# A two-layer hybrid trunk on one core: dense projections in pairs of k, a new price list for the order, first weights loaded earlier

## The chip, the cores and the metric

The kernel runs on one core of one Trainium2 chip. The metric is the device time of one execution in microseconds (us); lower is better. The kernel before takes 2569.01 us, the median of 3 runs (2567.93 to 2573.7).

The profile names the engines: PE is TensorE's matmul, PEld its weight load, DVE is VectorE, ACT is ScalarE, POOL is GpSimd and SP is SyncE, which issues the DMAs (SPq is its queue).

## The reference

The program is a trunk of two layers over 2048 positions of width 1024, in fp32. In each layer:

```python
h = rms_norm(x, norm_g[l]) * (1.0 + scale[:, None]) + shift[:, None]
proj = h @ w_in[l]
gq, gk, gv, glr, gz, dq, dk, dv, dz = split_columns(proj)
...
o_gla = gla_branch(gq, gk, gv, glr, gz, ...)      # 4 heads, linear attention by chunks of 64
o_diff = diff_branch(dq, dk, dv, dz, ...)         # 4 heads, two softmax maps, block-causal
y = jnp.concatenate([o_gla, o_diff], axis=-1) @ w_out[l]
x = x + gate[:, None] * y
```

`shift`, `scale` and `gate` come from `silu(c) @ w_ada[l] + b_ada[l]` and are called the modulation here. `gq`, `gk` and `gv` pass a causal convolution of 4 taps and a SiLU.

## The kernel before

**Units.** Each layer is cut into four units of 512 positions, u = 0 to 3. A unit has seven dense items, each of 8 k-tiles of 128 rows: items 0 to 3 are the four attention heads' projections (`proj_N`, the h tile is stationary), 4 and 5 the convolved inputs of the linear attention (`proj_T`, the weight is stationary), 6 its gate. Items 7 and 8 are the two halves of the output projection (`out_gen`). To keep fp32 accuracy with fast matmuls every operand is split into a high and a low part of type fp32r, and each product takes three matmuls: high by high, high by low, low by high. One k-tile of an item is 12 matmuls of 512 columns, an item is 96, and an item needs all four accumulator banks (`ps_a`, tiles named acc) until they are evacuated.

**Weights.** `weights()` gives the split weight of one k-tile in a tile w, of which there are four buffers (`p_w`). The first time (u = 0) the raw rows are loaded into tiles named raw, two k-tiles in one tile of the pool `p_kv` (5 buffers, shared with the keys Kj and Kt); ACT makes the high part, DVE the low part, and the result is kept in DRAM. Later units load the kept 512 KB (w<-wd).

**Attention.** For each of the four 128-row query tiles of a head: the scores (tiles sc, from Kj of earlier units and Kt of this one) are copied to s with a running minimum, ACT takes the exponential, DVE combines the two maps, PE transposes s (tp<-ident,s), ACT copies the transposes to aT, and PE multiplies aT by the values (po<-Vj,aT). At the end the four results are transposed (tp<-ident,z) and split into oh and ol for the output projection. A unit u works on u+1 blocks of keys, so u = 3 is the longest.

**Start.** `start()` loads the first layer's modulation weights in four chunks of 2 MB (`ada_load`, tiles wr) and turns each chunk, with the four x tiles, into two k-tiles of h (tp<-wr,cact, sc<-sel,t and tp<-ident,xt).

**What sets the order.** Generators (`dense_stream`, `attn_stream`, `gla_stream` and others) write the operations down in a program order. `Program.order()` then plays the program through with the durations of `cost()` and the latencies of `LAT`: an engine that is free takes, among the operations that are ready by these prices, the one that stands first in program order. The result is the fixed instruction order of each engine; on the chip an engine works through it in order and waits where something isn't ready. All instructions are issued at line 306 (`issue`), so the trace is read by tile names, not by lines.

In `dense_stream` the output projection of the unit before comes first, then the dense items of this one; for u = 0 they go in the order 0, 4, 1, 5, 2, 3, 6. `out_gen` takes the heads in the order

```python
for n_, k in enumerate((4, 5, 6, 0, 1, 2, 3, 7)):
    yield need("oT", key, 0 if k < 4 else k, lag=0.8)
```

so that 7 of its 8 k-tiles, 84 matmuls of the first half, need nothing of the last attention head (k = 7).

Of the kernel before, what the change touches and what calls it, by code (L numbers as in the profile page):

```python
# [11 lines left out]
F32 = mybir.dt.float32  # L12
# [15 lines left out]
EPS = 1e-6  # L28
NEG = -1e30
C_GQ, C_GV, C_GLR, C_GZ, C_D = 0, 512, 1024, 1040, 1552  # L30

# [87 lines left out]
class Program:  # L119
# [51 lines left out]
    @staticmethod  # L171
    def cost(e, method, args, kw, out):
        n = math.prod(out.shape[1:])
        if e == "S":
            return math.prod(out.shape) * 4 / 360.0
        if e == "T":
            if method == "transpose":
                return 110
            rate = {F32R: 2.4, BF16: 2.4, F32: 0.6}[args[2].dt]
            if rate == 0.6 and args[1].shape[1] < P:  # L180
                return 78
            return max(n / rate, 107 * args[1].shape[1] / P if rate == 2.4 else 216) + 3
        ins = [a for a in list(args[1:]) + list(kw.values()) if isinstance(a, View) and a is not kw.get("accum_out")]
        scalars = sum(math.prod(a.shape[1:]) == 1 for a in ins) if n > 1 else 0
        psum = any(a.buf.psum for a in ins)
        if method == "tensor_reduce":
            n = math.prod(ins[0].shape[1:])
        if e == "A":
            return 0.834 * n + (52 if psum else 93) + 93 * (scalars + ("accum_out" in kw))
        if e == "G":  # L190
            return 300 + 165 * n if kw.get("op") == ALU.pow else 100 + 2.2 * n
        fast = method in ("tensor_copy", "tensor_scalar") and not psum
        return (0.52 if fast else 1.042) * n + 68 + 61 * scalars

# [5 lines left out]
    def order(self):  # L200
# [25 lines left out]
        work, win = {}, 3413  # L226
        res, burst = [], 0
        while len(res) < N:
# [41 lines left out]
            elif e == "A" and self.table(ops[i]) not in (None, table):  # L270
                table = self.table(ops[i])
                free[e] = end = t + ops[i][5] + 1283
            elif e == "T":
                w = int(t / win)
                warm = work.get(w - 1, 0.0) > 0.5 * win
# [34 lines left out]
def trunk_kernel(ctx, tc, x, c, w_ada, b_ada, norm_g, w_in, conv_w, w_gk, b_gk, gla_norm_g,  # L310
# [238 lines left out]
    def pe(cost, wait=0.0):  # L549
        return ("pe", cost, wait)  # L550
# [34 lines left out]

    raws = {}

    def weights(l, u, item, k, src, n=None):
# [7 lines left out]
        if k % 2 == 0:  # L596
            raws[k // 2] = p_kv.tile([P, 2, 512], F32, tag="K", name="raw")
            for j in range(2):
                raw = raws[k // 2][:, j, :]
                SY.dma_start(raw if n is None else raw.rearrange("p (g n) -> p g n", n=n), src(k + j))  # L600
        raw = raws[k // 2][:, k % 2, :]
# [73 lines left out]
    def start():  # L675
# [6 lines left out]
        alloc_h()  # L682
        for c in range(4):
            if c < 3:
                wr.append(ada_load(c + 1))
            ada_first(c, wr[c])
            for pr in range(2):
                make_h(0, xs[2 * pr:2 * pr + 2], pr, c)
# [3 lines left out]
    def proj_T(l, u, item, col, banks):  # L692
        hhi, hlo = state["hhi"], state["hlo"]
        for k in range(KT):
            hi, lo = weights(l, u, item, k, lambda k: w_in[l, k * P:(k + 1) * P, col:col + 512])
            for j in range(4):
                cs = slice(j * P, (j + 1) * P)
                if k == 0:
                    banks.append(acc())
                T.matmul(banks[j], hi[:, cs], hhi[k], start=(k == 0), stop=False)  # L700
                T.matmul(banks[j], hi[:, cs], hlo[k], start=False, stop=False)
                T.matmul(banks[j], lo[:, cs], hhi[k], start=False, stop=(k == KT - 1))
                yield pe(0.65)

# [5 lines left out]
    def proj_N(load, banks):  # L710
        hhi, hlo = state["hhi"], state["hlo"]
        for k in range(KT):
            hi, lo = load(k)
            for t in range(TT):
                ts_ = slice(t * P, (t + 1) * P)
                if k == 0:
                    banks.append(acc())
                mm3(banks[t], hhi[k][:, ts_], hlo[k][:, ts_], hi, lo, k == 0, k == KT - 1)
                yield pe(0.65)

# [370 lines left out]
    def dense_gen(l, u, items):  # L1091
# [12 lines left out]
        def head_proj(hd):  # L1104
            def src(k):
                cols = w_in[l, k * P:(k + 1) * P, C_D:C_D + 2048].rearrange("p (g n) -> p g n", n=512)
                return cols[:, :, hd * P:hd * P + P]

            def ld(k):
                return weights(l, u, hd, k, src, n=P)  # L1110

            banks = []
            yield from proj_N(ld, banks)
            if hd == LAST:
# [34 lines left out]
    def out_gen(l, u):  # L1149
# [3 lines left out]
        final = key == L * NU - 1  # L1153
        yield need("ada", l, 2)
        for hf in range(2):
            cs = slice(hf * 512, hf * 512 + 512)
# [52 lines left out]
    def dense_stream():  # L1209
        order = (0, 4, 1, 2, 5, 3, 6)  # L1210
        prev = None
        for l in range(L):
            for u in range(NU):
                yield need("h", l * NU + u, lag=2.0)
                if prev:
                    yield from out_gen(*prev)
                yield from dense_gen(l, u, (0, 4, 1, 5, 2, 3, 6) if u == 0 else order)
                prev = (l, u)
# [47 lines left out]
```

## Time and profile before

| | |
|---|---|
| median of 3 runs | 2569.01 us |
| the profiled execution | 2571.75 us |
| its span, first to last instruction | 2570.0 us |
| PE busy | 2483.7 us (97%) |
| PEld busy | 2037.7 us (79%) |
| DVE busy | 1741.6 us (68%) |
| ACT busy | 1279.4 us (50%) |
| mean granted TensorE clock | 0.993 |
| DMA, mean over the span | 184 GB/s |

The stages stand on the time axis like this: start until about 32 us; layer 0, u = 0 until about 284; its units 1 to 3 until about 1284; the output projection of unit 3 until about 1340; layer 1, u = 0 until about 1540; its other units until 2540; the last 30 us are the rest of the last output projection. A matmul's recorded duration is longer than the distance to the next one's start, since matmuls are pipelined; so PE's busy share says where it clearly stood still, and hides short waits.

### The profile page before, as it was taken

The page shows a single profiled execution, that of the slowest core. Times are in us where ns is not written, and L with a number is a line of the kernel's source. Part 1 is how long each engine was busy: PE and PEld are TensorE (multiplying, and loading weights), DVE is VectorE, ACT ScalarE, POOL GpSimd, SP SyncE. Part 2 cuts the span into 40 slices and gives each one's busy share as a digit, 9 for nine tenths or more (in the row PEclk, how much of TensorE's full clock was granted, in tenths as well). Part 3 has the DMA queues.
Part 4 walks back from the last instruction along what each step waited for, and adds up shares of the span by engine and source line. Part 5 has one row for each costly group of instructions (what it writes and reads, how often), then busy time and mean ns, then how long its engine had stood idle before and what let it go on. Part 6 is the DMA issues. An engine that isn't in the chain of part 4 may idle for free.

```text
span 2570.0 us, 40465 instructions
## 1 busy us (share of the span) xinstructions
PE 2483.7 (97%) x13923; PEld 2037.7 (79%) x13923; DVE 1741.6 (68%) x5313; ACT 1279.4 (50%) x2760; POOL 139.7 (5%) x424
## 2 busy tenths in 40 slices
PE   8998999999999999999899999999999999999997
PEld 5776788777888878888777777888788888888886
DVE  4788777772777737677748883667637776377763
ACT  5556534562445624556625663445624556255532
POOL 0001000000000000000000010000000000000000
PEclk9999999999999999999999999999999999999998
DMA  8668866456453564434277567444464444643342
GB/s 257 236 225 289 300 232 219 132 187 228 149 189 101 187 212 146 141 131 167 94 260 264 214 226 260 161 165 173 145 237 160 145 154 150 229 138 129 108 147 90
DMA packets 204685, 474.00 MB, mean 184 GB/s; under 512 B 20736, under 2 KB 82368, under 8 KB 204480
## 3 DMA queue, kind: packets, MB, share of 16 engines
q1 hardware_dynamic: 204480, 471.41, 53.2%
q8 instruction: 111, 1.82, 0.3%
q14 instruction: 94, 0.77, 0.1%
HBM read 360.19 MB, written 111.15 MB: 183 GB/s over the span
## 4 chain that ended last, share of the span: by engine, by line
PE 76%; DVE 12%; ACT 6%; DMA 3%; issue 2%; SPq 1%; POOL 0%; ACTq 0%; POOLq 0%; DVEq 0%
PE acc L306 50%; PE sc L306 10%; PE po L306 9%; PE tp L306 7%; DVE s L306 5%; ACT qh L306 2%; DVE t L306 1%; ACT s L306 1%; DVE w L306 1%; DMA raw<-in_w_in_dram 1%; DVE ql L306 1%; DVE Kt L306 1%; ACT t L306 1%; ACT Kt L306 1%; SPq L306 1%
## 5 line engine op out<-in xcount | busy, mean ns | idle before, releaser
L306 PE MATMUL acc<-w,hhi 128*128 128x512 f32 x2560 | 831.3, 402 | 1.9 <-DVE w L306 1.1
L306 PEld LDWEIGHTS acc<-w,hhi 128*128 128x128 f32 x2560 | 465.1, 189 | 92.3 <-ACT ub L306 3.7
L306 PE MATMUL acc<-w,hlo 128*128 128x512 f32 x1280 | 505.3, 396 | 0.0
L306 ACT ACTIVATE s<-s,mx 128x256 f32<-128x256 f32 (+15 forms) x256 | 307.9, 1203 | 333.4 <-DVE s L306 328.9
L306 PE MATMUL acc<-hhi,w 128*128 128x512 f32 x1024 | 369.0, 404 | 0.2
L306 PE MATMUL acc<-w,oh 128*128 128x512 f32 x1024 | 334.3, 401 | 1.6 <-ACT oh L306 1.6
L306 DVE TENSOR_SCALAR_CACHE_REDUCE s<-sc,mx 64x64 f32<-64x64 f32 (+5 forms) x640 | 306.5, 485 | 35.7 <-PE sc L306 17.7
L306 PEld LDWEIGHTS acc<-w,hlo 128*128 128x128 f32 x1280 | 241.3, 188 | 49.2
L306 PEld LDWEIGHTS acc<-w,oh 128*128 128x128 f32 x1024 | 190.9, 190 | 42.9 <-issue 2.5
L306 PEld LDWEIGHTS acc<-hhi,w 128*128 128x128 f32 x1024 | 192.3, 189 | 38.4 <-DVE z L306 2.3
L306 PE MATMUL po<-Vj,aT 128*128 128x128 f32 x1536 | 209.5, 281 | 12.8 <-ACT aT L306 12.1
L306 PEld LDWEIGHTS po<-Vj,aT 128*128 128x128 f32 x1536 | 196.1, 196 | 25.4 <-ACT aT L306 19.0
L306 ACT COPY aT<-tp 128x512 f32<-128x512 f32 (+2 forms) x320 | 161.4, 520 | 104.6 <-PE tp L306 101.7
L306 PE MATMUL acc<-w,ol 128*128 128x512 f32 x512 | 202.7, 398 | 0.0
L306 PE MATMUL acc<-hlo,w 128*128 128x512 f32 x512 | 202.2, 395 | 0.0
L306 DVE SCALAR_TENSOR_TENSOR s<-s,r 128x512 f32<-128x512 f32 (+2 forms) x320 | 197.9, 668 | 3.4
L306 PE MATMUL tp<-ident,s 128*128 128x128 f32 x1088 | 174.0, 276 | 23.8 <-DVE s L306 7.8
L306 DVE TENSOR_SCALAR_CACHE_REDUCE s<-sc 128x512 f32<-128x512 f32 (+4 forms) x256 | 157.9, 622 | 55.5 <-PE sc L306 50.9
L306 PEld LDWEIGHTS tp<-ident,s 128*128 128x128 f32 x1088 | 131.4, 141 | 64.0 <-issue 24.7
L306 ACT COPY rw<-acc 128x256 f32<-128x256 f32 x128 | 50.3, 393 | 221.7 <-PE acc L306 220.5
L306 PE MATMUL sc<-Kj,qh 128*128 128x512 f32 x384 | 157.7, 411 | 2.2 <-DVE Kt L306 1.0
L306 ACT ACTIVATE qh<-tp,G 64x512 fp32r<-64x512 f32 x128 | 87.4, 683 | 128.3 <-PE tp L306 105.5
(183 smaller groups left out, 3708.5 us busy)
## 6 DMA issues: line engine op xcount, KB each, us to landing
w<-wd SPq DMA_DIRECT2D x424, 512.0 KB, 3.7
wd<-w SPq DMA_DIRECT2D x144, 512.0 KB, 4.2
raw<-in_w_in_dram SPq DMA_DIRECT2D x120, 256.0 KB, 5.3
Kj<-kd SPq DMA_DIRECT2D x48, 512.0 KB, 4.4
wr<-in_w_ada_dram SPq DMA_DIRECT2D x128, 128.0 KB, 2.8
kd<-Kt SPq DMA_DIRECT2D x24, 512.0 KB, 3.3
Vj<-vd SPq DMA_DIRECT2D x48, 256.0 KB, 3.5
wr<-in_w_ada_dram SPq DMA_DIRECT2D x8, 1024.0 KB, 11.9
```

The lines of the kernel that those rows point to most:

```text
L306: getattr(self.engines[e], method)(*[real(a) for a in args], **{k: real(v) for k, v in kw.items()})
```

## The change

Five things are edited.

- `proj_T` and `proj_N` take the k-tiles in pairs: the weights of two k-tiles are fetched first, then each of the four banks gets the six matmuls of both. `out_gen` keeps single k-tiles.
- `cost()` has other numbers, for PE, ACT and DVE (a surcharge for ACT and DVE operations on 64 partitions or fewer, among others), and `order()` adds time when PE changes between full-size matmuls and those of 64x64 or 32 columns.
- The raw weights of head 0, layer 0, are loaded in `start()`, one pair of k-tiles ahead of each later chunk of the modulation.
- In unit 3 of each layer the output projection stands in program order behind the last attention head (`need("attn", key, 3)`).
- The order of the items in u = 0 is 0, 1, 4, 5, 2, 3, 6, and in layer 1, u = 0, items 0 and 1 stand ahead of the output projection of layer 0's unit 3.

```diff
+KS = ((0, 1), (2, 3), (4, 5), (6, 7))
...
             rate = {F32R: 2.4, BF16: 2.4, F32: 0.6}[args[2].dt]
             if rate == 0.6 and args[1].shape[1] < P:
-                return 78
-            return max(n / rate, 107 * args[1].shape[1] / P if rate == 2.4 else 216) + 3
+                return 54 if args[1].shape[0] == CH else 60
+            return max(n * 0.444, 112 * args[1].shape[1] / P) if rate == 2.4 else max(n / rate, 216) + 6
...
+        half = 112 if out.shape[0] <= 64 and n > 16 else 0
...
-        return (0.52 if fast else 1.042) * n + 68 + 61 * scalars
+        return (0.52 if fast else 1.042) * n + 70 + 61 * scalars + half + 30 * ("accum_out" in kw)
...
+                if self.mode(ops[i]) != mode:
+                    mode = self.mode(ops[i])
+                    t += 160 if mode else 190
...
+    def load_raw(k, src, n):
+        raw = p_kv.tile([P, 2, 512], F32, tag="K", name="raw")
+        for j in range(2):
+            r = raw[:, j, :]
+            SY.dma_start(r if n is None else r.rearrange("p (g n) -> p g n", n=n), src(k + j))
+        return raw
...
         for c in range(4):
+            early[c] = load_raw(2 * c, head_src(0, 0), P)
             if c < 3:
                 wr.append(ada_load(c + 1))
             ada_first(c, wr[c])
...
     def proj_N(load, banks):
         hhi, hlo = state["hhi"], state["hlo"]
-        for k in range(KT):
-            hi, lo = load(k)
+        for ks in KS:
+            ws = [load(k) for k in ks]
             for t in range(TT):
                 ts_ = slice(t * P, (t + 1) * P)
-                if k == 0:
+                if ks[0] == 0:
                     banks.append(acc())
-                mm3(banks[t], hhi[k][:, ts_], hlo[k][:, ts_], hi, lo, k == 0, k == KT - 1)
-                yield pe(0.65)
+                for k, (hi, lo) in zip(ks, ws):
+                    mm3(banks[t], hhi[k][:, ts_], hlo[k][:, ts_], hi, lo, k == 0, k == KT - 1)
+                    yield pe(0.65)
...
         yield need("ada", l, 2)
+        if u == NU - 1:
+            yield need("attn", key, 3)
...
                 yield need("h", l * NU + u, lag=2.0)
+                items = (0, 1, 4, 5, 2, 3, 6) if u == 0 else order
+                ahead = 2 if l and u == 0 else 0
+                if ahead:
+                    yield from dense_gen(l, u, items[:ahead])
                 if prev:
                     yield from out_gen(*prev)
-                yield from dense_gen(l, u, (0, 4, 1, 5, 2, 3, 6) if u == 0 else order)
+                yield from dense_gen(l, u, items[ahead:])
```

The order that comes out of it differs on every engine. Three places are shown, each before and after. A name is a tile, without its number; x8 says that a row stands for eight equal ones.

The first is SP's queue at the start, from the small gate weights (t<-in_w_in_dram) on: wr are the modulation's chunks, raw the weights of head 0. Before:

```order
L306 DMA t_240<-in_w_in_dram 128x8x16
L306 DMA wr_245<-in_w_ada_dram 128x8x256
L306 DMA raw<-in_w_in_dram 128x4x128 x4
L306 DMA wr_282<-in_w_ada_dram 128x8x256
L306 DMA wr_314<-in_w_ada_dram 128x8x256
L306 DMA raw<-in_w_in_dram 128x4x128 x4
```

After:

```order
L319 DMA t_227<-in_w_in_dram 128x8x16
L319 DMA raw<-in_w_in_dram 128x4x128 x2
L319 DMA wr_248<-in_w_ada_dram 128x8x256
L319 DMA wr_260<-in_w_ada_dram 128x8x256
L319 DMA raw<-in_w_in_dram 128x4x128 x2
L319 DMA wr_307<-in_w_ada_dram 128x8x256
L319 DMA wr_347<-in_w_ada_dram 128x8x256
L319 DMA raw<-in_w_in_dram 128x4x128 x6
```

Two more raw loads stand further up, ahead of the second chunk. Before the last chunk (the last two rows of wr) four raw loads were issued, now six.

The second is PE at the end of layer 0, from the last score matmuls of head 3 of unit 3 on (sc are scores, tp<-ident,s the transposes, po the product with the values, acc the dense matmuls). Before:

```order
L306 MATMUL sc<-Kt,qh 128x512
L306 MATMUL sc<-Kt,ql 128x512
L306 MATMUL tp<-ident,s 128x128 x10
L306 MATMUL po<-Vj,aT 128x128 x4
L306 MATMUL tp<-ident,s 128x128 x4
L306 MATMUL po<-Vj,aT 128x128 x4
L306 MATMUL tp<-ident,s 128x128
L306 MATMUL po<-Vj,aT 128x128 x4
L306 MATMUL po<-Vt,aT 128x128 x3
L306 MATMUL tp<-ident,s 128x128 x8
```

After:

```order
L319 MATMUL tp<-ident,s 128x128 x8
L319 MATMUL acc<-w,hlo 128x512
L319 MATMUL acc<-w,hhi 128x512 x2
L319 MATMUL acc<-w,hlo 128x512
L319 MATMUL acc<-w,hhi 128x512 x2
L319 MATMUL acc<-w,hlo 128x512
L319 MATMUL acc<-w,hhi 128x512
L319 MATMUL tp<-ident,s 128x128 x3
L319 MATMUL po<-Vj,aT 128x128 x4
L319 MATMUL tp<-ident,s 128x128 x4
```

Matmuls of layer 1's head 0 (acc<-w,hhi and acc<-w,hlo) now stand between the attention's steps. From the one po<-Vt,aT that ends the first query tile's product to the last tp<-ident,z, PE had 15 dense matmuls in its row before, and has 71 now.

The third is PE at the end of the program, in the last attention head's last query tile; acc<-w,oh and acc<-w,ol are the last output projection. Before:

```order
L306 MATMUL sc<-Kt,qh 128x512
L306 MATMUL sc<-Kt,ql 128x512
L306 MATMUL tp<-ident,s 128x128 x12
L306 MATMUL po<-Vj,aT 128x128 x8
L306 MATMUL tp<-ident,s 128x128 x3
L306 MATMUL po<-Vj,aT 128x128 x4
L306 MATMUL po<-Vt,aT 128x128 x3
```

After:

```order
L319 MATMUL tp<-ident,s 128x128 x8
L319 MATMUL acc<-w,oh 128x512
L319 MATMUL acc<-w,ol 128x512
L319 MATMUL acc<-w,oh 128x512 x2
L319 MATMUL acc<-w,ol 128x512
L319 MATMUL acc<-w,oh 128x512 x2
L319 MATMUL acc<-w,ol 128x512
L319 MATMUL acc<-w,oh 128x512 x2
L319 MATMUL acc<-w,ol 128x512
L319 MATMUL acc<-w,oh 128x512 x2
L319 MATMUL acc<-w,ol 128x512
L319 MATMUL acc<-w,oh 128x512
```

Fifteen dense matmuls now stand between the eighth and the ninth transpose. From the first query tile's po<-Vt,aT to the last tp<-ident,z no dense matmul stood in the row before, and 45 stand there now; ahead of that place, in the same head, 84 stood before and 39 stand now. Behind it both have the same 108.

## Rows read from the trace of the kernel before

**Rows 1.** The page: busy time, share of the span and instructions of each engine; and the chain that ended last, as shares of the span.

```profile
PE 2483.7 (97%) x13923; PEld 2037.7 (79%) x13923; DVE 1741.6 (68%) x5313; ACT 1279.4 (50%) x2760; POOL 139.7 (5%) x424
...
PE 76%; DVE 12%; ACT 6%; DMA 3%; issue 2%; SPq 1%; POOL 0%; ACTq 0%; POOLq 0%; DVEq 0%
```

**Rows 2.** The stretches of the program: from:to in us, length, then the busy time (and instructions) of PE, PEld, DVE, ACT and, where it worked, POOL, then the granted PE clock, the DMA share and GB/s.

```profile
0.00:32.00 32.00, 19.98 (x148) 11.81 (x149) 13.38 (x57) 15.10 (x33) 3.57 (x14) 1.00 1.02 320
32.00:284.00 252.00, 238.70 (x1275) 187.32 (x1274) 204.55 (x634) 156.19 (x383) 18.45 (x54) 0.97 0.68 238
284.00:1240.00 956.00, 941.61 (x5363) 781.66 (x5362) 657.61 (x2003) 470.40 (x977) 48.07 (x146) 1.00 0.53 180
1240.00:1300.00 60.00, 53.42 (x302) 41.72 (x301) 32.41 (x89) 28.04 (x50) 3.01 (x10) 0.97 0.39 122
1300.00:1340.00 40.00, 40.00 (x180) 33.00 (x179) 16.79 (x40) 11.13 (x28) 0.00 (x0) 1.00 0.68 258
1340.00:1560.00 220.00, 205.48 (x1109) 160.71 (x1109) 185.08 (x553) 140.44 (x339) 19.13 (x52) 0.99 0.66 235
1560.00:2500.00 940.00, 928.35 (x5285) 775.94 (x5284) 605.75 (x1872) 442.38 (x926) 45.26 (x144) 1.00 0.48 166
2500.00:2540.00 40.00, 29.86 (x169) 24.40 (x168) 20.03 (x62) 15.73 (x27) 2.20 (x5) 0.87 0.04 14
2540.00:2570.00 30.00, 26.24 (x108) 21.17 (x108) 5.98 (x9) 0.00 (x0) 0.00 (x0) 0.94 0.55 193
```

**Rows 3.** Two pieces of the chain in order of time: start, length, what, count.

```profile
299.61 27.35 PE acc L306 x120
...
597.09 47.26 PE acc L306 x208
```

**Rows 4.** Who PE waited for, over the whole span: us in total, times, longest.

```profile
PE sc L306 <- DVE Kt L306: 16.8, 18, 2.2
PE po L306 <- ACT aT L306: 15.2, 14, 3.1
```

**Rows 5.** PE's timeline at the start: start, length, instruction, count, in brackets the idle time before and its releaser.

```profile
31.46 2.31 PE L306 MATMUL acc<-w,hhi 128*128 128x512 f32 x5
...
40.20 1.07 PE L306 MATMUL tp<-wr,cact 128*32 128x256 f32 x16
...
42.90 0.53 PE L306 MATMUL tp<-ident,xt 128*128 128x128 f32 x3
```

**Rows 6.** SP's queue in the same stretch: start, length of the issues, what, count.

```profile
20.99 5.14 SPq L306 DMA_DIRECT2D raw<-in_w_in_dram  x4
26.23 4.14 SPq L306 DMA_DIRECT2D wr<-in_w_ada_dram  x2
```

**Rows 7.** PE waiting for Kt in two stretches, from 32 to 284 us and from 1340 to 1560 us, as in rows 4.

```profile
PE sc L306 <- DVE Kt L306: 7.1, 5, 2.2
...
PE sc L306 <- DVE Kt L306: 5.2, 5, 2.0
```

**Rows 8.** PE's timeline around one such wait: the last transposes of rw, which start the making of Kt, the last dense matmul, and the first score matmul.

```profile
193.16 0.88 PE L306 MATMUL tp<-ident,rw 128*128 128x128 f32 x6
...
197.09 0.39 PE L306 MATMUL acc<-w,hlo 128*128 128x512 f32 x1
199.34 0.33 PE L306 MATMUL sc<-Kt,qh 128*128 128x128 f32 x1 [1.86 <-DVE Kt L306]
```

**Rows 9.** PE's timeline at the end of layer 0.

```profile
1254.60 0.40 PE L306 MATMUL acc<-w,ol 128*128 128x512 f32 x1
1256.48 0.66 PE L306 MATMUL tp<-ident,s 128*128 128x128 f32 x4 [1.48 <-ACT aT L306]
...
1260.54 0.71 PE L306 MATMUL po<-Vt,aT 128*128 128x128 f32 x4 [1.30 <-ACT aT L306]
...
1283.31 0.33 PE L306 MATMUL tp<-ident,z 128*128 128x128 f32 x1 [1.04 <-DVE z L306]
1284.42 1.22 PE L306 MATMUL acc<-w,oh 128*128 128x512 f32 x2 [0.78 <-ACT oh L306]
```

**Rows 10.** The first 80 us of layer 1's u = 0, columns as in rows 2.

```profile
1340.00:1420.00 80.00, 73.03 (x355) 58.41 (x355) 67.20 (x206) 45.07 (x111) 5.88 (x20) 1.00 0.79 273
```

**Rows 11.** PE's timeline at the end of the program.

```profile
2498.58 0.39 PE L306 MATMUL acc<-w,ol 128*128 128x512 f32 x1
...
2504.16 1.78 PE L306 MATMUL tp<-ident,s 128*128 128x128 f32 x12 [0.53 <-DVE s L306]
2508.92 3.02 PE L306 MATMUL po<-Vj,aT 128*128 128x128 f32 x16 [2.98 <-ACT aT L306]
...
2524.19 3.78 PE L306 MATMUL po<-Vj,aT 128*128 128x128 f32 x16 [3.15 <-ACT aT L306]
...
2538.74 0.33 PE L306 MATMUL tp<-ident,z 128*128 128x128 f32 x1 [1.51 <-DVE z L306]
2539.84 1.55 PE L306 MATMUL acc<-w,oh 128*128 128x512 f32 x4 [0.78 <-ACT oh L306]
```

**Rows 12.** DMA issues from 284 to 2500 us: count, KB each, median us from issue to landing.

```profile
w<-wd SPq DMA_DIRECT2D x419, 512.0 KB, 3.7
...
Kj<-kd SPq DMA_DIRECT2D x48, 512.0 KB, 4.4
```

More of the change, by code (lines that the diff above doesn't have):

```diff
@@ L188, in cost @@
         if e == "A":
-            return 0.834 * n + (52 if psum else 93) + 93 * (scalars + ("accum_out" in kw))
+            return 0.834 * n + (45 if psum else 85) + 93 * (scalars + ("accum_out" in kw)) + half
         if e == "G":
@@ L192, in cost, with mode @@
         fast = method in ("tensor_copy", "tensor_scalar") and not psum
-        return (0.52 if fast else 1.042) * n + 68 + 61 * scalars
+        return (0.52 if fast else 1.042) * n + 70 + 61 * scalars + half + 30 * ("accum_out" in kw)
+    @staticmethod
+    def mode(op):
+        if op[1] == "transpose" or op[2][2].dt != F32:
+            return 0
+        k, m = op[2][1].shape
+        return 1 if (k, m) == (CH, CH) else 2 if m == 32 else 0
     @staticmethod
@@ L584, in run_streams, with head_src, src @@
                 clock[0] = max(min(nxt), clock[0]) + 1e-6
-    raws = {}
+    raws, early = {}, {}
+    def load_raw(k, src, n):
[4 more added lines that the diff above has]
+        return raw
+    def head_src(l, hd):
+        def src(k):
+            cols = w_in[l, k * P:(k + 1) * P, C_D:C_D + 2048].rearrange("p (g n) -> p g n", n=512)
+            return cols[:, :, hd * P:hd * P + P]
+        return src
     def weights(l, u, item, k, src, n=None):
@@ L596, in weights @@
         if k % 2 == 0:
[L597 to L600, printed above, removed]
+            raws[k // 2] = early.pop(k // 2) if k // 2 in early else load_raw(k, src, n)
         raw = raws[k // 2][:, k % 2, :]
@@ L693, in proj_T @@
         hhi, hlo = state["hhi"], state["hlo"]
-        for k in range(KT):
-            hi, lo = weights(l, u, item, k, lambda k: w_in[l, k * P:(k + 1) * P, col:col + 512])
+        for ks in KS:
+            ws = [weights(l, u, item, k, lambda k: w_in[l, k * P:(k + 1) * P, col:col + 512]) for k in ks]
             for j in range(4):
                 cs = slice(j * P, (j + 1) * P)
-                if k == 0:
+                if ks[0] == 0:
                     banks.append(acc())
-                T.matmul(banks[j], hi[:, cs], hhi[k], start=(k == 0), stop=False)
-                T.matmul(banks[j], hi[:, cs], hlo[k], start=False, stop=False)
-                T.matmul(banks[j], lo[:, cs], hhi[k], start=False, stop=(k == KT - 1))
-                yield pe(0.65)
+                for k, (hi, lo) in zip(ks, ws):
+                    T.matmul(banks[j], hi[:, cs], hhi[k], start=(k == 0), stop=False)
+                    T.matmul(banks[j], hi[:, cs], hlo[k], start=False, stop=False)
+                    T.matmul(banks[j], lo[:, cs], hhi[k], start=False, stop=(k == KT - 1))
+                    yield pe(0.65)
     def mm3(bank, ahi, alo, hi, lo, first, last):
@@ L711, in proj_N @@
         hhi, hlo = state["hhi"], state["hlo"]
-        for k in range(KT):
-            hi, lo = load(k)
+        for ks in KS:
+            ws = [load(k) for k in ks]
             for t in range(TT):
                 ts_ = slice(t * P, (t + 1) * P)
-                if k == 0:
+                if ks[0] == 0:
                     banks.append(acc())
-                mm3(banks[t], hhi[k][:, ts_], hlo[k][:, ts_], hi, lo, k == 0, k == KT - 1)
-                yield pe(0.65)
+                for k, (hi, lo) in zip(ks, ws):
+                    mm3(banks[t], hhi[k][:, ts_], hlo[k][:, ts_], hi, lo, k == 0, k == KT - 1)
+                    yield pe(0.65)
     def to_oT(blocks, gain):
@@ L1104, in head_proj @@
         def head_proj(hd):
[L1105 to L1110, printed above, removed]
             banks = []
-            yield from proj_N(ld, banks)
+            yield from proj_N(lambda k: weights(l, u, hd, k, head_src(l, hd), n=P), banks)
             if hd == LAST:
```

2 lines of the change are left out of this document (1 added, 1 removed).

## The prediction

> **What bounds the kernel.** I read the page's busy shares first: PE 97%, and PE carries 76% of the chain that ended last [rows 1]. So the kernel is bound by TensorE, and the matmuls of the reference, the same 12,187 in both orders, set a floor that the change can't move. What it can move is PE's standing still. The second view is the table of stretches [rows 2]: the length of a stretch less PE's busy time is its plain idle time. That gives 12.0 us in the first 32, 13.3 in layer 0's first unit (32 to 284), 14.4 in 284 to 1240, 6.6 at the layer boundary (1240 to 1300), none in 1300 to 1340, 14.5 in layer 1's first unit (1340 to 1560), 11.7 in 1560 to 2500, 10.1 in 2500 to 2540 and 3.8 behind it: 86 us in all. The reader is to see that the losses sit in four short places and hardly in the long middle.
>
> The third view is the chain in order of time: 120 dense matmuls in 27.35 us, 208 in 47.26, so 0.227 us each at full rate [rows 3]. I price a dense matmul that fills a gap at that. Since the recorded duration is longer than this distance, waits shorter than about 0.2 us don't show as idle; the true loss is larger than 86 us, by how much no view says. The last view is who PE waited for: Kt, the split key, 18 times with 16.8 us, and aT, the copied transposes, 14 times with 15.2 us [rows 4]. In both the fixed order has put PE at an instruction whose operand comes later than the price list thought, with too few dense matmuls ahead of it.
>
> **Start.** Before the last chunk's transposes (until 43.4 us, [rows 5]) PE's row holds 26 dense matmuls before and 44 now, so 18 x 0.227 = 4.1 us of work is done earlier. Against it, two more raw loads stand ahead of the last modulation chunk. SP's queue took 5.14 us for four of them [rows 6], 1.28 each, so the chunk comes 2.6 us later; by the mean rate of the stretch, 320 GB/s [rows 2], 0.52 MB take 1.6 us. Net 1.5 to 2.5 us gained; I take 2. The ends are 4.1 gained (the later chunk is covered) and 2.6 lost (PE has no gap there for the earlier matmuls).
>
> The raw rows of a head arrive in pieces of 512 bytes, and their four issues held the queue for 5.14 us [rows 6]. The Trainium skill (Perfetto Trace Analysis, DMA Optimizations) says that transfers under 2 KB carry a significant overhead each, which speaks against putting them ahead of the modulation. By that rule the price is the 2.6 and the term 1.5; by the mean rate it is 1.6 and the term 2.5.
>
> **Layer 0, first unit.** Here every weight is split on ACT and DVE, and DVE is busy 204.6 of 252 us [rows 2]. 7.1 of the 13.3 idle us are five waits for Kt [rows 7]. In the shown one the transposes start at 193.16 and the first score at 199.34, with dense matmuls only until 197.09 [rows 8]. Counting the matmul time that each order puts between a head's last rw transpose and its first score, the four heads had 2.0, 2.0, 3.4 and 2.8 us and have 2.0, 3.2, 4.1 and 2.7. So the new prices (a surcharge for operations on 64 partitions, as Kt's are) give back 1.8 us, not 7. With the other waits of the stretch I take 3 gained. Ends: 7.1 gained, and 5 lost if the two heads in a row, 0 and 1, crowd DVE.
>
> **Layer boundary.** In 1240 to 1300 PE stands still 6.6 us. The dense matmuls that need nothing of the last head run out near 1254.60; behind it come the waits of 1.48 and 1.30 us for aT, and at the end 1.04 for z and 0.78 for oh [rows 9]. The order now has 71 dense matmuls in this piece where it had 15: 56 x 0.227 = 12.7 us of filler for 4.8 us of idle (the 6.6 less the last two waits, which also shrink since layer 1's matmuls stand there). The granted clock of the stretch is 0.97 [rows 2], so some 3.6 of its 60 us went at the lower level. I take 6 gained, between nothing (the filler itself waits for its raw weights) and 8.4.
>
> **Layer 1, first unit.** Idle 14.5 us, 7.0 of them in its first 80 us [rows 2, 10], where heads 0 and 1 begin. Their weights are now split during unit 3's attention, where DVE is busy 54% and, to 1340, 42%, not 84% [rows 2], and the output projection, whose weights are kept ones, is left as filler for these two heads. I take the 7.0, between 10 gained and 2 lost (the splits get in the way of unit 3's attention).
>
> **End of the program.** From 2498.58 to 2539.84 no dense matmul stands in PE's row; it waits 2.98 and 3.15 us for aT and shorter ones beside them [rows 11], 10.1 us in 2500 to 2540. The order now has 45 dense matmuls there, 10.2 us, taken from the piece ahead, where 84 stood and 39 are left. The waits of 1.51 for z and 0.78 for oh stay, since the 108 matmuls behind them need the last head. So up to 7.9 us can be filled; I take 7. The granted clock is 0.87 in these 40 us and 0.94 in the next 30 [rows 2]: about 10.4 and 3.6 us at 1.2 GHz in place of 2.4, at most 7 us of loss. With fewer gaps I take back 2 of it. Together 9, between 4 (the piece ahead, with half its filler, begins to wait) and 14.9.
>
> In the 40 us with the granted clock of 0.87, PE stood still twice for about 3 us [rows 2, 11]. The Trainium skill (TensorE: Matmul & The Clock Gate, Part 1) says that the lower clock is the default and activity lifts it. By that rule filled gaps would keep the clock up and the term is nearer 14; if the clock falls as often as before, it is 7.
>
> **The middle.** In the other units the orders are nearly alike. Kt's remaining waits are 16.8 - 7.1 - 5.2 = 4.5 us [rows 4, 7], and the orders give the heads of the second units 0.4 to 0.9 us more before the score: 2 gained. The pairs cost something. A buffer w was free for 36 dense matmuls, 8.2 us, before its next content was needed; now, at the tightest, for 27, 6.1 us, and two loads start at nearly the same time. One lands in 3.7 us [rows 12]; the second's 512 KB take another 2.0 at 258 GB/s in 1300 to 1340 [rows 2]: 5.7, just inside. Of the 168 pairs with kept weights some 55 have less than 7 us of PE work in between. I take 1 lost, between nothing and 33 (55 pairs, each 0.6 late, if a load takes the 4.4 that Kj takes [rows 12]). Longer runs on one bank and the later release cost nothing else that I see: the four banks are evacuated at an item's end as before.
>
> **Sum.** 2 + 3 + 6 + 7 + 9 + 2 - 1 = 28 us gained. The profiled execution took 2571.75 (span 2570.0 and 1.75 around it), so its like would take 2543.8; it lies 2.7 above the median of 2569.0, so a median of 2541. The single execution and the median straddle 2542, which I forecast.
>
> **Rivals.** A: the chains set the time. The waits for aT and Kt are latencies of DVE and ACT work; if the filler delays the attention's own steps as much as it fills, the idle moves and doesn't go. For it: the tail's filler is taken from matmuls that were already hiding such waits. Against it: PE had no idle time ahead of 2498. Then only the start, a third of the tail and a few us elsewhere remain, 10 gained: 2559.
>
> B: more than the visible waits go. Short waits that the busy time hides are as wrongly priced as the long ones, and the new prices shorten them everywhere. For it: in the first units the idle shares are largest where DVE is fullest. Against it: the middle's order hardly changed. If as much again as the 28 is found there, less a few: 2519.
>
> C, slower: weights land late in the pairs. SP's queue is in order, and a load that waits for its buffer holds up the keys and values behind it. If half of the 168 pairs wait 0.6 us, 50 are lost against 29 gained: 2590. It decides from 0.17 us per pair on average (29 / 168). For it: the margin is 0.4 or less. Against it: between most pairs attention work stands, which gives the load more than 7 us, and before no wait of note was for w.
>
> D: the edits cancel. The new order is as far from the chip's timing as the old one, gaps close in one place and open in another: 2569.
>
> **Chances.** Forecast (2525 to 2554) 0.60, A 0.15, B 0.08, C 0.10, D 0.07. About 0.2%, 5 us, is what a measurement here tells from no change. Faster by more than that: the forecast, B and most of A, 0.82; no change: D and the rest of A, 0.08; slower 0.10. The range that leaves out C, D and the far half of B is 2519 to 2564.
>
> **What would show it.** Right: PE's idle time in the last 70 us falls from 13.9 to about 7 and dense matmuls stand between the last transposes; near the layer boundary acc<-w,hhi stands between the po rows and PE idles under 3 us; layer 1's first unit idles about 7; the Kt waits fall to about 12. Wrong: new waits of PE for w or for its DMA, above all in units 1 to 3; a first dense matmul at the start that isn't earlier; or waits for aT as long as before with the filler ahead of them.

## The result, and the profile after

The changed kernel takes 2538.49 us (median of 4 runs, 2537.81 to 2540.38); beside it the kernel before took 2568.47 (2565.19 to 2573.7). The ratio is 0.9883, 95% interval 0.9865 to 0.9900: 30 us faster, by 26 to 35. The profiled execution took 2537.81, its span is 2536.1.

The page, PE's busy time and the chain, as in [rows 1]:

```profile
PE 2471.4 (97%) x13923; PEld 2028.9 (80%) x13923; DVE 1738.6 (69%) x5313; ACT 1287.2 (51%) x2760; POOL 137.2 (5%) x424
...
PE 78%; DVE 11%; ACT 5%; DMA 4%; issue 2%; SPq 0%; POOL 0%; ACTq 0%; POOLq 0%; DVEq 0%
```

The spans differ by 33.9 us, and it splits in two. PE's idle time (span less busy) fell from 86.3 to 64.7, by 21.6. Its busy time fell by 12.3 for the same 13,923 instructions. Most of that goes with the clock, by an estimate: the mean granted clock went from 0.993 to 0.997, and span times what is missing of 1 is 18.0 us before and 7.6 after.

The stretches, columns as in [rows 2], cut at about the same places of the program:

```profile
0.00:29.00 29.00, 18.34 (x114) 11.08 (x115) 13.20 (x55) 12.91 (x26) 3.29 (x12) 1.00 1.00 312
29.00:284.00 255.00, 238.50 (x1310) 185.97 (x1309) 205.18 (x638) 159.03 (x390) 19.26 (x56) 0.98 0.69 240
284.00:1205.00 921.00, 911.73 (x5189) 756.98 (x5188) 628.22 (x1909) 450.61 (x933) 45.40 (x141) 1.00 0.53 182
1205.00:1245.00 40.00, 33.65 (x172) 24.58 (x171) 37.05 (x113) 28.73 (x60) 2.73 (x7) 0.96 0.24 80
1245.00:1324.00 79.00, 77.56 (x446) 64.58 (x445) 55.18 (x183) 51.67 (x119) 6.05 (x20) 1.00 0.50 170
1324.00:1534.00 210.00, 201.66 (x1085) 162.51 (x1084) 157.95 (x461) 113.09 (x266) 14.13 (x40) 1.00 0.74 261
1534.00:2455.00 921.00, 915.64 (x5204) 760.43 (x5203) 601.45 (x1840) 445.13 (x928) 43.58 (x140) 1.00 0.49 168
```

By the work done, 1205 us after is where the kernel before stands at 1207 and not at the 1240 of [rows 2]. So the kernel before once more, cut there:

```profile
284.00:1207.00 923.00, 909.97 (x5189) 756.37 (x5188) 626.21 (x1907) 445.96 (x930) 46.04 (x141) 1.00 0.54 181
1207.00:1240.00 33.00, 31.65 (x176) 25.28 (x175) 31.40 (x96) 24.44 (x49) 2.03 (x5) 1.00 0.42 141
1207.00:1340.00 133.00, 125.06 (x653) 100.00 (x652) 80.60 (x224) 63.61 (x127) 5.04 (x15) 0.99 0.48 168
```

Length less PE's busy time gives the idle time of each:

| stage | idle before | idle after |
|---|---|---|
| start | 12.0 | 10.7 |
| layer 0, first unit | 13.3 | 16.5 |
| layer 0, units 1 to 3 (to 1207 and 1205) | 13.0 | 9.3 |
| layer boundary (to 1340 and 1324) | 7.9 | 7.8 (6.4 of it in 1205 to 1245) |
| layer 1, first unit | 14.5 | 8.3 |
| layer 1, units 1 to 3 | 11.7 | 5.4 |
| last 70 us | 13.9 | 6.7 |

The last line is from stretches of 70 us in both; the others are from the rows. The reader is to see that the end, layer 1 and the later units of layer 0 gained, that layer 0's first unit lost, and that the boundary's idle time moved forward by some 40 us and did not go.

Who PE waited for, as in [rows 4]:

```profile
PE sc L319 <- DVE Kt L319: 9.5, 11, 2.6
PE tp L319 <- DVE s L319: 8.7, 11, 2.4
...
PE po L319 <- ACT aT L319: 2.2, 4, 1.1
PE acc L319 <- DMA w<-wd: 2.1, 4, 0.7
```

Kt fell from 16.8 to 9.5 us and aT from 15.2 to 2.2. The wait for w's load is new and small.

PE's timeline at the end of the program, the place of [rows 11]:

```profile
2488.69 1.03 PE L319 MATMUL tp<-ident,s 128*128 128x128 f32 x8
2489.48 0.47 PE L319 MATMUL acc<-w,oh 128*128 128x512 f32 x1
...
2493.01 0.60 PE L319 MATMUL tp<-ident,s 128*128 128x128 f32 x4
2493.36 0.48 PE L319 MATMUL acc<-w,oh 128*128 128x512 f32 x1
2493.80 2.05 PE L319 MATMUL po<-Vj,aT 128*128 128x128 f32 x16
...
2505.47 0.33 PE L319 MATMUL tp<-ident,z 128*128 128x128 f32 x1 [1.51 <-DVE z L319]
2506.57 1.20 PE L319 MATMUL acc<-w,oh 128*128 128x512 f32 x4 [0.78 <-ACT oh L319]
```

Where PE stood 2.98 and 3.15 us before a po, dense matmuls now stand. The two waits behind the last head are as long as before, to the hundredth.

PE's timeline at the layer boundary:

```profile
1217.13 0.45 PE L319 MATMUL acc<-w,hlo 128*128 128x512 f32 x1
1218.00 0.50 PE L319 MATMUL sc<-Kj,qh 128*128 128x512 f32 x1 [0.42 <-DVE s L319]
...
1228.66 0.63 PE L319 MATMUL sc<-ident,xt 128*128 128x128 f32 x4
1231.19 1.69 PE L319 MATMUL tp<-ident,s 128*128 128x128 f32 x8 [1.90 <-DVE s L319]
1232.53 0.78 PE L319 MATMUL acc<-w,hhi 128*128 128x512 f32 x1
```

ACT in the same place (hhi is the high part of h; each cast makes 256 of a k-tile's 512 columns):

```profile
1202.43 0.62 ACT L319 CAST w<-raw 128x512 fp32r<-128x512 f32 x1
...
1216.04 0.75 ACT L319 CAST hhi<-t 128x256 fp32r<-128x256 f32 x2
...
1231.24 0.70 ACT L319 CAST hhi<-t 128x256 fp32r<-128x256 f32 x2
...
1240.46 0.70 ACT L319 CAST hhi<-t 128x256 fp32r<-128x256 f32 x2
...
1242.68 0.62 ACT L319 CAST w<-raw 128x512 fp32r<-128x512 f32 x1 [1.24 <-PE acc L319]
```

The same casts of the second half of h in the kernel before, first and last:

```profile
1236.79 0.71 ACT L306 CAST hhi<-t 128x256 fp32r<-128x256 f32 x2
...
1242.87 0.71 ACT L306 CAST hhi<-t 128x256 fp32r<-128x256 f32 x2
```

From 1217.13 to 1232.53 there is no dense matmul. Layer 1's head 0 stands there in place of the output projection. Of its 48 matmuls on the first half of h, 24 are done, those of the first four k-tiles. The four buffers w hold these k-tiles' weights until the second half of h is there, so ACT makes no further w between 1202.43 and 1242.68. And the second half of h is made only between 1231 and 1241, among the attention's exponentials. In the kernel before it was made no earlier, but the output projection stood in PE's row meanwhile, and PE was idle for 1.4 us in 1207 to 1240.

### The profile page after: what moved, and what is told of

Same layout as the page of the kernel before. It is cut to its first block, busy times and chain, and to the rows that moved or that the text cites. A ratio compares the mean times of both kernels' runs of the same rounds, so it can differ in the third digit from the quotient of the medians.

```text
span 2536.1 us, 40517 instructions
## 1 busy us (share of the span) xinstructions
PE 2471.4 (97%) x13923; PEld 2028.9 (80%) x13923; DVE 1738.6 (69%) x5313; ACT 1287.2 (51%) x2760; POOL 137.2 (5%) x424
## 4 chain that ended last, share of the span: by engine, by line
PE 78%; DVE 11%; ACT 5%; DMA 4%; issue 2%; SPq 0%; POOL 0%; ACTq 0%; POOLq 0%; DVEq 0%
PE acc L319 50%; PE sc L319 12%; PE po L319 9%; PE tp L319 7%; DVE s L319 3%; ACT qh L319 2%; DVE t L319 1%; DMA wr<-in_w_ada_dram 1%; DMA w<-wd 1%; DVE ql L319 1%; DMA raw<-in_w_in_dram 1%; ACT s L319 1%; ACT t L319 1%; DVE vN L319 1%; DMA Kj<-kd 1%
## 5 line engine op out<-in xcount | busy, mean ns | idle before, releaser
L319 PE MATMUL acc<-w,hhi 128*128 128x512 f32 x2560 | 842.4, 404 | 3.4 <-ACT w L319 1.9
L319 ACT ACTIVATE s<-s,mx 128x512 f32<-128x512 f32 (+15 forms) x256 | 308.3, 1205 | 304.9 <-DVE s L319 302.7
L319 PE MATMUL acc<-hhi,w 128*128 128x512 f32 x1024 | 362.8, 401 | 1.0 <-DMA w<-wd 1.0
L319 PE MATMUL po<-Vj,aT 128*128 128x128 f32 x1536 | 204.1, 277 | 0.8 <-ACT aT L319 0.5
L319 PEld LDWEIGHTS po<-Vj,aT 128*128 128x128 f32 x1536 | 190.3, 192 | 10.7 <-ACT aT L319 4.9
L319 PEld LDWEIGHTS tp<-ident,s 128*128 128x128 f32 x1088 | 132.1, 141 | 52.4 <-issue 12.9
```

The costliest lines, as they stand in the source:

```text
L319: getattr(self.engines[e], method)(*[real(a) for a in args], **{k: real(v) for k, v in kw.items()})
```

## The experiments

Each kernel was timed in turn with the kernel before, and its ratio is to that. In the third column the ratio is set against the changed kernel's 0.9883, times 2571 us (about the median of the kernel before beside these runs). The changed kernel itself wasn't timed beside them, and its ratio is known to 0.0018: an error there moves the whole column by up to 4.5 us in one direction.

| run | ratio, 95% interval | us against the changed kernel | median, range |
|---|---|---|---|
| e1_before_tail | 0.9956 (0.9942 to 0.9971) | (11.3 below before) | 2559.29, 2555.15 to 2562.03 |
| e2_after_no_tail | 0.9928 (0.9912 to 0.9943) | +11.6 | 2552.47, 2546.79 to 2556.38 |
| e3_single_k | 0.9932 (0.9917 to 0.9947) | +12.6 | 2551.53, 2548.96 to 2555.28 |
| e6_boundary_undone | 0.9895 (0.9880 to 0.9909) | +3.1 | 2542.73, 2541.91 to 2545.09 |
| e7_last_pair | 0.9875 (0.9860 to 0.9890) | -2.1 | 2539.44, 2535.86 to 2541.87 |
| e8_no_last_pair | 0.9895 (0.9879 to 0.9910) | +3.1 | 2543.79, 2539.83 to 2549.24 |
| e4_old_prices | 0.9933 (0.9920 to 0.9946) | +12.9 | 2553.05, 2549.95 to 2558.42 |
| b1_out_pair | 0.9866 (0.9852 to 0.9879) | -4.4 | 2536.36, 2534.93 to 2539.41 |
| e5_no_early | 0.9876 (0.9862 to 0.9891) | -1.8 | 2540.61, 2540.00 to 2542.11 |
| e9_old_items | 0.9872 (0.9856 to 0.9888) | -2.8 | 2539.12, 2536.19 to 2544.62 |
| c1_nudge | 0.9899 (0.9882 to 0.9915) | +4.1 | 2546.88, 2546.19 to 2549.04 |
| r1_nudge_single | 0.9938 (0.9924 to 0.9951) | +14.1 | 2555.56, 2552.03 to 2559.12 |

### The end of the program: the rule alone, and all but the rule

e1, the kernel before with the rule for its last unit:

```diff
         yield need("ada", l, 2)
+        if final:
+            yield need("attn", key, 3)
```

> The kernel before with one line of the change: in the last unit of layer 1 alone the output projection stands behind the last attention head. Nothing ahead of 2430 us is edited. My theory (filler: dense matmuls between the attention's steps take the place of the waits for aT, and PE, kept at work, keeps its clock) expects 13 to 16 us less than before, about 2554, the granted clock of the last 70 us near 1.00, and no wait for aT over 1 us there. Rival 1 (the clock falls in the tail whatever stands there; only idle time is filled) expects 6 to 8 us less, about 2562, and a clock of 0.90 or below. Rival 2 (the chain of DVE and ACT work sets the tail; filler taken from the piece ahead only moves the waits) expects 0 to 3 us less, with new waits between 2440 and 2500 us.

e2, the changed kernel without it there:

```diff
-        if u == NU - 1:
+        if u == NU - 1 and not final:
             yield need("attn", key, 3)
```

> The changed kernel without that one line for the last unit (it stays in layer 0). The filler theory expects 13 to 16 us more than the changed kernel, about 2553, with the two waits of about 3 us for aT back and the clock of the last 70 us at 0.87 to 0.94 again. Rival 1 (only idle time) expects 6 to 8 us more, about 2546. Rival 2 (the tail's gain came from the new prices, which order the last head's steps better) expects less than 3 us more, about 2540.

Alone, the rule takes 11.3 us off the kernel before (7.5 to 14.9 by the interval); without it the changed kernel is 11.6 slower. PE's timeline of e2 shows the old waits again, and the stretch ahead of e1's last 70 us shows what the moved filler leaves behind:

```profile
2488.52 3.48 PE L319 MATMUL po<-Vj,aT 128*128 128x128 f32 x16 [2.98 <-ACT aT L319]
...
2503.63 2.05 PE L319 MATMUL po<-Vj,aT 128*128 128x128 f32 x16 [3.19 <-ACT aT L319]
```

```profile
2440.00:2487.40 47.40, 47.29 (x285) 40.45 (x284) 37.42 (x110) 23.03 (x39) 2.51 (x9) 1.00 0.45 150
```

PE is idle for 0.1 us there, so rival 2 falls: the dense matmuls taken from there were not needed. In the last 70 us:

| | idle | granted clock |
|---|---|---|
| before | 13.9 | 0.90 |
| e1 | 6.2 | 0.98 |
| e2 | 14.0 | 0.98 |
| after | 6.7 | 1.00 |

The idle time follows the rule in both pairs, by 7.7 and 7.3 us. The clock is less regular: 7.0, 1.4, 1.4 and 0 us of the 70 by this table. With the same gaps, e2's profiled execution lost 5.6 us less to the clock than before's, and the mean clock of e2's six executions went from 0.993 to 0.998. So of the measured 11.5 us 7 to 8 are idle time, and the rest, some 4, goes with the clock: by the means of all executions, 0.9953 in e2 and 0.9965 in the changed kernel, it is 3. My expected 13 to 16 took before's one execution for the rule.

### Single k-tiles

```diff
-KS = ((0, 1), (2, 3), (4, 5), (6, 7))
+KS = ((0,), (1,), (2,), (3,), (4,), (5,), (6,), (7,))
```

> The changed kernel with single k-tiles in place of pairs in proj_T and proj_N; all else stays. My prediction put the pairs at 1 us of cost, so it expects 2536 to 2540, the four short waits for w gone. Rival 1 (the pairs are what gained the 4.7 us in the middle of layer 1, by longer runs on one bank) expects 2543 or more. Rival 2 (late weights, up to 33 us hidden in short waits) expects 2525 or less.

12.6 us slower: the pairs are a gain, and not the small cost of the prediction. One place is plain, the end of layer 1's unit 1. ACT's timeline there, first the changed kernel, then e3 (s<-s,mx is an exponential, t<-acc the first step in emptying a bank of the unit's last item):

```profile
1787.61 1.05 ACT L319 ACTIVATE s<-s,mx 128x896 f32<-128x896 f32 x1 [1.09 <-DVE s L319]
...
1788.65 0.58 ACT L319 ACTIVATE t<-acc 128x512 f32<-128x512 f32 x1
...
1791.67 0.58 ACT L319 COPY aT<-tp 128x512 f32<-128x512 f32 x1
```

```profile
1801.02 0.57 ACT L319 COPY aT<-tp 128x512 f32<-128x512 f32 x1
1801.49 1.09 ACT L319 ACTIVATE t<-acc 128x512 f32<-128x512 f32 x2
```

In the changed kernel the first bank is emptied 3.0 us ahead of the copy aT<-tp, so the next item's matmuls stand behind the transposes and fill the wait. With singles the banks are emptied behind that copy, and PE waits 2.56 us for aT, as in the kernel before. That suggested a theory: with a pair at the end, an item's first bank gets its last matmul 18 matmuls before the item's end, not 9, and comes free earlier.

### Which pair, and one more

e7 and e8:

```diff
-KS = ((0, 1), (2, 3), (4, 5), (6, 7))
+KS = ((0,), (1,), (2,), (3,), (4,), (5,), (6, 7))
```

> The changed kernel with single k-tiles 0 to 5 and only the last two, 6 and 7, as a pair. With singles throughout the time was 11 to 13 us above the changed kernel's. Theory (bank release): in the last pair bank 0 gets its last matmul 18 dense matmuls, 4.1 us, before the item's end, and 9 matmuls, 2.0 us, with singles; so its evacuation is done by when the next item wants the bank. It expects nearly all of the pairs' gain kept: 0 to 4 us above the changed kernel, 2538 to 2543. Rival 1 (the gain is from longer runs of each weight pair or from fewer loads at odd times, anywhere in the item) expects 8 to 10 us above, since six of eight k-tiles are single: about 2548. Rival 2 (any other order differs by chance) expects 4 to 12 us above without a pattern at the item ends.

```diff
-KS = ((0, 1), (2, 3), (4, 5), (6, 7))
+KS = ((0, 1), (2, 3), (4, 5), (6,), (7,))
```

> The reverse: k-tiles 0 to 5 in three pairs, 6 and 7 single. The bank release theory expects the gain of the pairs gone: 8 to 13 us above the changed kernel, about 2549, with PE waiting at the unit's end for aT by some 2.5 us as with singles throughout, and no dense matmul of the next item ahead of that wait. Rival 1 (gain spread over the pairs) expects 2 to 4 us above, about 2541.

b1, the output projection's second half with a last pair too:

```diff
-            for n_, k in enumerate((4, 5, 6, 0, 1, 2, 3, 7)):
+            for n0, ks in ((0, (4,)), (1, (5,)), (2, (6,)), (3, (0,)), (4, (1,)), (5, (2,))) + (((6, (3, 7)),) if hf else ((6, (3,)), (7, (7,)))):
```

> The changed kernel with one more pair: the last two k-tiles of the output projection's second half (k 3 and 7) go bank by bank as well. The bank release theory expects a gain at the eight places where a dense item follows a second half: 11 to 13 us over some 56 item ends is 0.2 us per end, so 1 to 3 us less than the changed kernel, about 2537. Rival 1 (here the next item is held by h or weights, not by its banks) expects no difference within 1 us. Rival 2 (its weights for k 7 wait for the last head and hold k 3 up) expects 1 to 4 us more.

The last pair alone keeps the whole gain (e7), as the theory said and rival 1 did not. But without it e8 loses 3.1 us and not 8 to 13, as rival 1 said, so neither fits both. And the place shown above goes against the theory: e7, with the last pair, has the wait of 2.55 us for aT there, and e8, without it, has none. b1 has the lowest median of all; its interval overlaps the changed kernel's, so it is not shown to be better.

### A control, and the pairs once more

```diff
-            return max(n * 0.444, 112 * args[1].shape[1] / P) if rate == 2.4 else max(n / rate, 216) + 6
+            return max(n * 0.446, 112 * args[1].shape[1] / P) if rate == 2.4 else max(n / rate, 216) + 6
```

> A control: the changed kernel with one price moved by less than half a per cent (0.446 ns per column for a fast matmul, in place of 0.444). No theory gives this a cost. It tells how far the time moves by another order alone: if it stays within 2 us of the changed kernel, differences of 4 us or more between the other runs are effects of their edits; if it moves by 5 us or more, only the sites shown in the traces can be believed.

r1 has the same line and the single k-tiles of e3.

> The control's price (0.446) with single k-tiles: the effect of the pairs once more, in another order. Singles were 11 to 13 us above the changed kernel, and the price alone moved it by 4 to 8 us. Theory (the pairs carry the 12 us, by early release of the banks or in another way) expects 8 to 13 us above the control, 2555 to 2560, and the losses near item ends up by 4 us or more over the control's. Rival (the singles' loss was a chance of the order, as the control's own) expects 2544 to 2552, within 5 us of the control, with its losses elsewhere than the singles' at the first price.

Another order with no reason behind it is 4.1 us slower by the ratio, where the intervals overlap, and 8.4 by the medians, which weren't taken side by side. So e5, e6, e7, e8, e9 and b1, all within 4.4 us, can't be judged by their times; only by places in their traces. The pairs stand: singles cost 12.6 us at one price and 10.0 at the other (0.9938 less 0.9899, times 2571), and in both the intervals are apart. PE's waits for the emptying of a bank (ub, z, t and rt are read from banks), in e3:

```profile
PE acc L319 <- ACT ub L319: 1.9, 5, 0.8
...
PE acc L319 <- DVE z L319: 1.3, 3, 0.5
```

and in r1:

```profile
PE acc L319 <- DVE rt L319: 4.7, 1, 4.7
PE acc L319 <- ACT ub L319: 2.7, 6, 1.0
PE acc L319 <- DVE t L319: 1.1, 3, 0.6
PE acc L319 <- DVE z L319: 1.0, 1, 1.0
```

With t's 0.2 in e3 that is 3.4 and 9.5 us; the same names give 0.6 in the changed kernel and 1.0 in the control. The 4.7 for rt in r1 isn't the pairs': it comes behind an output projection, at 318 us, whose k-tiles are single in every kernel here but b1, and e4, which has the pairs, waits 3.3 us for rt at 321. Without it singles wait longer for their banks by 2.8 us in e3 and by 3.8 in r1. That is no account of the 12.6 and 10.0. Other waits are shorter there, and PE's idle time over the whole span (span less busy) is only 3.3 us longer in e3 than in the changed kernel (68.0 to 64.7) and 1.1 longer in r1 than in the control (71.5 to 70.4). Most of the loss stands in PE's busy time, 7.8 and 9.0 us; of e3's some 3 us go with the clock (0.996 to 0.997 in the profiles), of r1's none that these figures show (0.995 in both). So that pairs gain is shown, and by what is not.

### The prices

```diff
-            return max(n * 0.444, 112 * args[1].shape[1] / P) if rate == 2.4 else max(n / rate, 216) + 6
+            return max(n / rate, 107 * args[1].shape[1] / P if rate == 2.4 else 216) + 3
...
-        half = 112 if out.shape[0] <= 64 and n > 16 else 0
...
-                if self.mode(ops[i]) != mode:
-                    mode = self.mode(ops[i])
-                    t += 160 if mode else 190
```

> The changed kernel with the numbers of cost() as before and without the added time between PE's forms of matmul; all other edits stay. Theory (the prices shorten the waits for Kt, 16.8 us before and 9.5 after, and little else) expects 5 to 9 us above the changed kernel, about 2546, with the Kt waits back at about 15 us. Rival 1 (the prices do nothing; the Kt waits went with the items' other order) expects within 2 us. Rival 2 (the prices also carry the middle's and the first units' short waits) expects 15 us or more above, 2554.

12.9 us slower, between the theory and rival 2. The Kt waits are back:

```profile
PE sc L315 <- DVE Kt L315: 16.0, 14, 3.4
```

That is 6.5 us over the changed kernel, near all of the fall from 16.8, and half of the loss. The idle time of the whole span is 77.1 (2550.5 less 2473.4), 12.4 above the changed kernel's.

### The boundary, the start and the items

e6:

```diff
-                ahead = 2 if l and u == 0 else 0
+                ahead = 0
...
-        if u == NU - 1:
+        if final:
             yield need("attn", key, 3)
```

> The changed kernel with the order of programs at the layer boundary as before: layer 0's last output projection neither waits for the last head nor stands behind layer 1's items 0 and 1; the tail keeps its rule. My theory (the filler at the boundary and the early splits for layer 1's first unit gained 1.9 and 9.7 us) expects 10 to 13 us more than the changed kernel, about 2550, with the waits for aT near 1255 us back and the new dip at 1217 to 1237 us gone. Rival 1 (the first unit's gain comes from the new prices, not from the move) expects 0 to 3 us more, about 2540. Rival 2 (the dip costs as much as the move gains) expects no difference or less time, 2530 to 2538.

By time it is within what the control moved. By stretches the idle time moves back: 0.9 us in 1203 to 1233 (the dip is gone), 7.1 in 1233 to 1320 (the waits for aT are back), 12.1 in layer 1's first unit (1320 to 1538). The sum is 20.1, against 16.1 for the changed kernel in 1205 to 1534. So the move gave some 4 us in layer 1's first unit and about nothing at the boundary.

e5:

```diff
-            early[c] = load_raw(2 * c, head_src(0, 0), P)
```

> The changed kernel without the early loads: head 0's raw weights of layer 0 are loaded as in the kernel before, behind the modulation's chunks. The prediction's term expects 2 us more than the changed kernel, about 2541. The traces so far show some 3 us gained by the time the first 30 us of PE work are done, with half or all of it given back within the next 70; rival 1 (given back) expects within 1 us, 2539. Rival 2 (the early loads delay the modulation's last chunk by the 2.6 us of their issues) expects 1 to 3 us less.

The same time within 2 us. PE's first dense matmul in the changed kernel and the last chunk's transposes, for [rows 5]:

```profile
21.45 1.22 PE L319 MATMUL acc<-w,hhi 128*128 128x512 f32 x2
...
41.46 1.07 PE L319 MATMUL tp<-wr,cact 128*32 128x256 f32 x16
```

The first dense matmul is 10 us earlier than before, the last chunk 1.3 us later (40.20 in [rows 5]; in e5 it is at 39.98), nearer to the 1.6 of the mean rate than to the 2.6 of the issues. The Trainium skill (Perfetto Trace Analysis, DMA Optimizations) says that transfers under 2 KB carry a significant overhead each; by that rule it was 2.6, and this trace doesn't bear it out. The gain shows early and is soon gone: at 46 us the changed kernel has 50 dense matmuls behind it and the kernel before 38, at 80 us both have 144, and at 284 us 738 and 739.

e9:

```diff
-                items = (0, 1, 4, 5, 2, 3, 6) if u == 0 else order
+                items = order if u else (0, 1, 4, 5, 2, 3, 6) if l else (0, 4, 1, 5, 2, 3, 6)
```

> The changed kernel with the items of layer 0's first unit in the order of before, 0, 4, 1, 5, 2, 3, 6; layer 1's first unit keeps the new one. With the old prices this unit lost 8 us more PE time than in the changed kernel, and with the new prices it still loses 3 us more than before the change, low clock taken out in each. Theory (heads 0 and 1 in a row crowd DVE, which splits their weights and makes their keys): the old order gives 3 to 8 us back, 2531 to 2536. Rival 1 (the loss is from the early start, not from the items) expects within 2 us. Rival 2 (the two heads in a row give attention work earlier, which fills the unit) expects 2 us more or worse.

PE's idle time from 29 to 284 is 16.4 us, against 16.5 in the changed kernel: two heads in a row are not what costs layer 0's first unit.

## Why the prediction was right, point by point

The time was forecast at 2542 and is 2538.5, by a sum of 28 that came out as 30. The sum hides errors of both signs: by idle time the start, layer 0's first unit and the boundary, put at 11 gained, lost 1.8, and the middle, put at 1, gained 10.0. That they cancel is luck. The prediction's reading that the losses were "hardly in the long middle" was wrong by its own list, where 26.1 of the 86 us stand there. (Its 12,187 matmuls stand in no view; the page has 13,923 instructions of PE in both kernels.)

- **End, 9: right, and for its reason.** The idle part was put at 7 and is 7.2 (7.7 and 7.3 in the two pairs with one line between them). The two waits that were to stay, 1.51 and 0.78, stayed. The clock part, 2, was too small: some 4 on average, 7 between the two profiles. The Trainium skill (TensorE: Matmul & The Clock Gate, Part 1) says that activity lifts the clock; by that rule the term was 14, and this pair of traces agrees, 1.00 for 0.90. But e2 shows the same gaps at 0.98, so gaps alone don't set it.
- **Layer 1, first unit, 7: right in size, and in part for its reason.** Idle time 14.5 to 8.3, Kt waits there 5.2 to 2.4. e6 puts some 4 of it on the move that was to give all; the rest comes with the other edits.
- **Layer boundary, 6: wrong.** The step that failed is "56 x 0.227 = 12.7 us of filler". I counted dense matmuls and asked only whether their raw weights would be there; those of the first four k-tiles were split in time. Their other operand, the second half of h of the next unit, wasn't there, and the four buffers w were full until it was. The output projection, which needs no h, had covered the making of h in the kernel before, and the change took this cover away. Idle time went from 7.9 to 7.8; the waits of [rows 9] for aT are gone and those at the new dip stand in their place.
- **Layer 0, first unit, 3, and start, 2: wrong.** The early matmuls came, and the Kt waits fell by 1.7 us (7.1 in [rows 7] to 5.4), near the 1.8 that the count of filler gave. The step that failed is taking these as gained: other waits took the time, and nothing of the 5 was left at 284, where the idle time is 27.2 us and was 25.3. e4, e5 and e9 undo one edit each and none brings it back; the cause stays open.
- **Middle, 2 less 1: wrong in sign for the pairs.** The step is "longer runs on one bank and the later release cost nothing else that I see: the four banks are evacuated at an item's end as before". Pairs in place of singles gain 10 to 13 us where 1 was to be lost. That an item's banks end one after the other, and farther apart with pairs, is one thing that this step left out; it shows in 2.8 and 3.8 us of waits, and where the rest comes from stays open. The other part, the prices' 2 for Kt, is small beside the 10.0 us of idle time that the middle gained. The bound of 33 us for late weights didn't come near: the waits are 2.1 us, though w's loads took a median of 4.0 us and Kj's 6.0 in these units, longer than in [rows 12].
- **The prices** were given 2 us in the middle and 1.8 in the first unit; undoing them costs 12.9, three times the control.

Of the rivals, C fell with the waits for w, A with the end, D with the ratio. B was partly true: the units in the middle lost 10.0 us of idle time with an order that looked nearly the same.

The edits don't add up: end 11.6, pairs 12.6, prices 12.9 and boundary 3.1 make 40, not 30. Taken out singly, each also takes the others' fit with it.

## What to carry to other kernels

When work is moved into a gap, check every operand of the moved work at its new time, and what the work that stood there had been covering. Where a schedule is a fixed order, take a control first, one price moved by half a per cent: here it moved the time by 4 to 8 us, and any smaller effect can only be read from a place in the trace. And before a longer wait is called the cause of a loss, set it against the change of the whole idle time: with single k-tiles the waits for banks grew, and the idle time hardly did.

## What the runs showed of the hardware that was not expected

The clock can make most of one kernel's spread. e8's lowest run, 2539.83 us, had a mean granted clock of 0.999, its highest, 2549.24, had 0.995: 0.004 of 2545 is 10.2 us, the difference is 9.4. It isn't all of every spread: two executions of the kernel before at 0.995, timed with e1, took 2570.78 and 2574.21.

Between the two profiles about 10 of the 33.9 us go with the clock, which was lower in several short places of the kernel before (0.97, 0.87 and 0.94 in [rows 2]), although PE was 97% busy in both. Over more executions it is less: the mean clock is 0.9943 in 36 executions of the kernel before, timed with the experiments, and 0.9965 in the four of the changed one, some 6 us of the 30. What sets where the clock falls isn't shown; the gaps alone don't, as e2's end has them at 0.98.
